# A hybrid attention layer on one core: the first projection step by token tile, and one output projection moved out of the merge

## The chip, the cores and the metric

The kernel runs on one core of a Trainium2 chip. The metric is the device time of one execution in microseconds (us), the median over the runs shown. The engines are TensorE (PE in the profile; its weight loads, which overlap its matmuls, are PEld), VectorE (DVE), ScalarE (ACT), GpSimd (POOL) and SyncE (SP), whose queue issues most of the loads. SBUF is the on-chip memory, PSUM the banks that TensorE writes.

## What is computed

One layer with two attention branches over 256 latent tokens (x) and 256 context tokens (ctx), width 2048, everything in fp32:

```python
hc = modulate(rms_norm(ctx, norm1_g), m_ctx[0], m_ctx[1])    # shift and scale from c_ctx
h  = modulate(rms_norm(x,   norm1_g), m_lat[0], m_lat[1])    # shift and scale from c
ka, va, kb, vb = keys and values of hc and of h, by w_in[:, :3072]
qa, qb, ga, gb = split_qg(h @ w_in[:, 3072:], q_norm_a, q_norm_b)
oa = gqa(qa, ka, va)                       # branch a: 16 heads of 128, 4 of keys
ob = diff_attn(qb, kb, vb, lam, ...)       # branch b: 8 heads, p0 - lam * p1
merged = sigmoid(ga) * (oa @ w_br_a) + sigmoid(gb) * (ob @ w_br_b)
x = x + m_lat[2] * (merged @ w_out)
x = x + m_lat[5] * swiglu(modulate(rms_norm(x, norm2_g), m_lat[3], m_lat[4]))
```

`m_lat` and `m_ctx` are six chunks of `silu(cond) @ w_ada + b_ada`. The scalar `lam` comes from four short vectors.

## The kernel before

**Products.** Each fp32 product is made of three fp32r products (`mm3`, L209): high part by high, high by low, low by high. `load_w` (L196) brings a weight tile of 256 rows by 512 columns (in the first steps 128 rows) through SP's queue into one of 7 buffers `wraw`; ScalarE casts the high part `whi` (L205), VectorE subtracts to get the low part `wlo` (L206). Activations are split in the same way (`split`, L214). One weight tile feeds 12 matmuls of 128x512 where there are two token tiles, 24 where there are four.

**The start.** The 512 tokens are four token tiles of 128 (indices 0 and 1 are the context, 2 and 3 are x). Each token tile lies in four column quarters `tok` of 512. The loads go in this order: x (both tiles at once, four DMAs), two small vectors, `w_ada` for the first shift and scale, the first weight tile, then the context (four DMAs). `row_norm` (L133) takes squares of the four quarters (for tiles 2, 3 and 0 on ScalarE, for tile 1 on VectorE), sums them and scales all four quarters by the root (the power is POOL's, L130). `ada_cond` (L249) makes shift and scale for a step by matmuls with 32 rows (L266) and a transpose (L275). `modulated` (L292) transposes a step's token columns (`xtp`, L306), applies scale and shift (`hx`), and splits. `kv_group` (L321) multiplies with `w_in`.

The key and value projection of all 512 tokens runs over six steps of 1, 1, 2, 4, 4 and 4 rows of tiles of `w_in` (`steps`, L492), and in each step over the six column groups 2, 3, 0, 4, 5, 1 (kb0, kb1, ka, vb0, vb1, va). In the first step both x tiles of column group 2 stand ahead, then both context tiles, then the other groups. The next step's shift and scale are made between the groups that `BATCH` (L491) names.

**Work on the side.** `later` (L468) makes the other chunks of the conditioning: per piece a load of 0.5 MB on SP's queue and a rank-one product on VectorE (`ada`, L364) that is ordered behind the latest `wlo`. `keys` and `values_a` normalise and rotate keys, and split values; `tables` (L174) makes the tables for the rotation and, at its end, the six operations for `lam` and `gsub`.

**Attention.** 16 units of branch b and 16 of branch a. A unit's front half makes scores and softmax, its back half the transposed probabilities and outputs. Between the halves `filler` (L703) feeds weight tiles of other projections, by `take` and by a count `pieces` of tiles against a goal (L744 and L752): six groups of q and eight groups of gates, whose results go to DRAM (`gate_d`) through POOL's queue. After every weight tile of the filler `side_work` (L692) does this:

```python
    turns[0] += 1
    if turns[0] % 2:
        take(later, 1)
    take(chores[-1], 1)
```

so that a piece of `later` comes every second tile, beside a piece of the chores (the keys of branch a and its values). The second tile of b's keys is made ahead of unit 8 (L734), with two tiles of filler per piece.

**The merge.** For each of four column groups (L760): the loads of b's two gates and their sigmoids, the projection of b's outputs (`w_brb`, 4 weight tiles), the loads of a's gates and sigmoids, the projection of a's outputs (`w_bra`, 8 weight tiles); `gated` (L781) multiplies and adds, `turn` (L782) transposes the sum. At each odd tile a piece of `later` is taken. The raw attention outputs are split by `o_parts` (L571), four heads at a time: for branch b (4, 5) ahead of the merge, for branch a (0 to 3) during it. Then follow `w_out`, the second norm and the feed-forward part, which the change does not touch.

## Time and profile before

| | |
|---|---|
| median of 3 runs | 1750.39 us (1748.45 to 1753.29) |
| the profiled execution, its own time | 1752.44 us |
| its span in the profile | 1750.7 us |
| TensorE busy | 1709.3 us, 98% of the span |
| VectorE, ScalarE, POOL busy | 1128.9 us (64%), 773.2 us (44%), 126.5 us (7%) |
| granted clock of TensorE, mean | 0.993 |
| DMA, mean over the span | 225 GB/s |

Busy time is the union of an engine's instructions over one span. The granted clock is the share of TensorE's full clock (1.00 is 2.4 GHz, 0.50 is 1.2 GHz). A matmul row's duration overlaps those of its neighbours in the pipeline, so the pace is read from the starts of two that follow each other. In brackets behind a row of the timeline stands the idle time ahead of it and what released the instruction. In the chain of work that ended last TensorE has 88%, VectorE 5%.

### The profile page before, as it was taken

Reading aid. Unit: us, or ns where it says so; the run is one execution under the profiler, and the core shown is the slowest. Engines: PE = TensorE matmul, PEld = TensorE weight load, DVE = VectorE, ACT = ScalarE, POOL = GpSimd, SP = SyncE. Lnnn points to the kernel's source line nnn. Section 1 sums busy time; section 2 is a strip of 40 time slices with the busy share of each in tenths; the row PEclk is TensorE's granted clock in tenths of the full one; section 3 lists DMA queues with packets and bytes.
Section 4 is the critical chain, followed back from the end, with each engine's and each line's share of the span. In section 5 each row is a group of like instructions: output and inputs, shape, how many; then the busy total and the mean of one; then the engine's idle time right before and its main releaser. Section 6 shows DMA issues by size and latency. Waiting matters only on the chain.

```text
span 1750.7 us, 21655 instructions
## 1 busy us (share of the span) xinstructions
PE 1709.3 (98%) x8106; PEld 1378.3 (79%) x8106; DVE 1128.9 (64%) x1416; ACT 773.2 (44%) x1061; POOL 126.5 (7%) x188
## 2 busy tenths in 40 slices
PE   5999999999999999999999999999999999999998
PEld 3767778887877788878888878888888888888887
DVE  4754658888798786968556664555566555454554
ACT  4422223246655566575444454444444444333332
POOL 2100001001132200001000100000000000000000
PEclk8999999999999999999999999999999999999999
DMA  9867785687776665648786756677777777666662
GB/s 271 281 222 262 239 306 181 195 269 246 223 231 222 204 236 175 212 133 278 245 288 225 251 176 190 203 239 233 238 239 239 234 237 232 208 197 214 219 204 90
DMA packets 190600, 393.47 MB, mean 225 GB/s; under 512 B 13120, under 2 KB 25488, under 8 KB 189984
## 3 DMA queue, kind: packets, MB, share of 16 engines
q1 hardware_dynamic: 183824, 369.71, 65.2%
q0 software_dynamic: 6672, 22.39, 4.1%
q8 instruction: 63, 1.03, 0.2%
q14 instruction: 41, 0.34, 0.1%
HBM read 383.62 MB, written 8.42 MB: 224 GB/s over the span
## 4 chain that ended last, share of the span: by engine, by line
PE 88%; DVE 5%; issue 3%; DMA 2%; ACT 1%; POOL 1%; SPq 1%; ACTq 0%; DVEq 0%; POOLq 0%
PE mm L211 27%; PE mm L210 26%; PE mm L212 26%; PE ada L266 2%; DVE wlo L206 1%; DMA wraw<-in_w_in_dram 1%; PE ptp L646 1%; PE s L626 1%; PE o L664 1%; ACT whi L205 1%; PE ftp L902 1%; DVE ada L364 0%; PE o L211 0%; DMA wada<-in_w_ada_dram 0%; PE o L210 0%
## 5 line engine op out<-in xcount | busy, mean ns | idle before, releaser
L206 DVE TENSOR_TENSOR wlo<-wraw,whi 128x1024 fp32r<-128x1024 f32 (+1 forms) x506 | 611.0, 1210 | 472.0 <-ACT whi L205 471.6
L205 ACT CAST whi<-wraw 128x1024 fp32r<-128x1024 f32 (+1 forms) x506 | 527.2, 1043 | 800.1 <-PE mm L212 685.4
L211 PE MATMUL mm<-wlo,hT 128*128 128x512 f32 x696 | 271.0, 389 | 2.0 <-DVE rstd L129 2.0
L210 PE MATMUL mm<-whi,hT 128*128 128x512 f32 x696 | 272.8, 392 | 0.0
L212 PE MATMUL mm<-whi,hT 128*128 128x512 f32 x696 | 271.2, 390 | 0.1
L210 PE MATMUL mm<-whi,xT 128*128 128x512 f32 x640 | 257.8, 407 | 2.3 <-ACT xT L215 1.8
L211 PE MATMUL mm<-wlo,xT 128*128 128x512 f32 x640 | 254.7, 398 | 4.9 <-DVE wlo L206 4.9
L212 PE MATMUL mm<-whi,xT 128*128 128x512 f32 x640 | 252.9, 395 | 0.0
L211 PEld LDWEIGHTS mm<-wlo,hT 128*128 128x128 f32 x696 | 130.7, 188 | 28.8 <-DVE wlo L206 2.4
L212 PEld LDWEIGHTS mm<-whi,hT 128*128 128x128 f32 x696 | 130.6, 188 | 27.7 <-DVE hT L216 0.5
L210 PEld LDWEIGHTS mm<-whi,xT 128*128 128x128 f32 x640 | 121.5, 190 | 39.3 <-issue 9.3
L364 DVE SCALAR_TENSOR_TENSOR ada<-wada,sc,ada 128x1024 f32<-128x1024 f32 x120 | 152.1, 1278 | 0.0
L210 PEld LDWEIGHTS mm<-whi,hT 128*128 128x128 f32 x696 | 130.7, 188 | 26.5
L211 PEld LDWEIGHTS mm<-wlo,xT 128*128 128x128 f32 x640 | 122.2, 191 | 30.5 <-DVE wlo L206 6.4
L212 PEld LDWEIGHTS mm<-whi,xT 128*128 128x128 f32 x640 | 122.0, 191 | 25.6
L210 PE MATMUL mm<-whi,fT 128*128 128x512 f32 x352 | 137.2, 390 | 0.0
L212 PE MATMUL mm<-whi,fT 128*128 128x512 f32 x352 | 137.0, 389 | 0.0
L211 PE MATMUL mm<-wlo,fT 128*128 128x512 f32 x352 | 136.9, 389 | 0.0
L210 PEld LDWEIGHTS mm<-whi,fT 128*128 128x128 f32 x352 | 66.1, 188 | 14.6 <-issue 0.8
L211 PEld LDWEIGHTS mm<-wlo,fT 128*128 128x128 f32 x352 | 66.1, 188 | 13.7
L212 PEld LDWEIGHTS mm<-whi,fT 128*128 128x128 f32 x352 | 66.1, 188 | 13.6
L210 PE MATMUL mm<-whi,cT 128*128 128x512 f32 x192 | 75.9, 395 | 0.4 <-ACT cT L215 0.4
(226 smaller groups left out, 2089.5 us busy)
## 6 DMA issues: line engine op xcount, KB each, us to landing
wada<-in_w_ada_dram SPq DMA_DIRECT2D x192, 512.0 KB, 4.5
wraw<-in_w_in_dram SPq DMA_DIRECT2D x154, 512.0 KB, 4.7
wraw<-in_w_ff_gate_dram SPq DMA_DIRECT2D x88, 512.0 KB, 4.2
wraw<-in_w_ff_up_dram SPq DMA_DIRECT2D x88, 512.0 KB, 4.1
wraw<-in_w_ff_down_dram SPq DMA_DIRECT2D x88, 512.0 KB, 4.8
wraw<-in_w_br_a_dram SPq DMA_DIRECT2D x32, 512.0 KB, 4.9
wraw<-in_w_out_dram SPq DMA_DIRECT2D x32, 512.0 KB, 5.2
wraw<-in_w_br_b_dram SPq DMA_DIRECT2D x16, 512.0 KB, 5.7
```

The lines of the kernel that those rows point to most:

```text
L205: nc.scalar.copy(out=hi[:, 0:nk], in_=raw[:, 0:nk])
L206: last_lo.append(nc.vector.tensor_tensor(out=lo[:, 0:nk], in0=raw[:, 0:nk], in1=hi[:, 0:nk].bitcast(F32), op=ALU.subtract))
L210: nc.tensor.matmul(ps, lhsT=ah, rhs=wh, start=first, stop=False)
L211: nc.tensor.matmul(ps, lhsT=ah, rhs=wl, start=False, stop=False)
L212: nc.tensor.matmul(ps, lhsT=al, rhs=wh, start=False, stop=last)
L266: nc.tensor.matmul(aps[32 * g:32 * g + 32, 0:ncol], lhsT=cst[:, k, :], rhs=rhs, start=(k < 4), stop=(k >= NKT - 4))
L364: nc.vector.scalar_tensor_tensor(out=dst, in0=wt, scalar=sc[:, 0, kt:kt + 1], in1=dst, op0=ALU.mult, op1=ALU.add)
L626: nc.tensor.matmul(sps[i], lhsT=qT[rows, x, hh, tk * P:(tk + 1) * P], rhs=kT["b", grp][y][rows, hh, :], start=(n == 0), stop=(n == 2))
L646: nc.tensor.transpose(out=tp[:, kt * P:(kt + 1) * P], in_=p[:, kt * P:(kt + 1) * P], identity=ident)
L664: nc.tensor.matmul(op[:, 0:BV], lhsT=pT[:, kt, :], rhs=vb[:, kt, hh * BV:(hh + 1) * BV], start=(kt == 0), stop=(kt == 3))
L902: nc.tensor.transpose(out=tp[:, j * P:(j + 1) * P], in_=act[tk][:, j * P:(j + 1) * P], identity=ident)
```

## The change

1. **Loads.** The two small vectors and `w_ada` go first; then each token tile by itself (four DMAs of 128x512), with weight tiles of groups 2, 3 and 0 between them.
2. **The first step by token tile.** `row_norm` now squares quarters 0 and 2 on ScalarE, 1 and 3 on VectorE, and returns the root; `row_scale` scales the quarters named: first only quarter 0, which the first step needs, and the others behind the split. `mod_first` transposes, modulates and splits one token tile; `kv_first` multiplies it with one of the column groups 2, 3, 0 and copies the result out. Groups 4, 5, 1 of the first step go as before. `BATCH[0]` is (3, 4) instead of (0, 2).
3. **Unread products.** `keep_busy` puts transposes of the identity into a PSUM bank that nobody reads: 16 before and 10 after the transposes of the first token tile, 8 and 10 around those of the second.
4. **`lambdas`.** The six operations for `lam` and `gsub` are ordered behind the `wlo` that is the latest when the fifth step begins.
5. **Side work.** A chore goes first; a piece of `later` only where there is no chore and no `quiet` (set while b's second keys are made), and then every second tile, every third once a's keys and values are done.
6. **The differential projection** (`w_br_b`) is no longer in the merge. It is the last part of the filler, behind the gates (`others`); its results go to DRAM (`prod_d`). The splits of b's outputs are done as it starts, those of a's first three groups behind a's units.
7. **The merge** has a's projection only. `load_gated` takes one step after each weight tile: it loads b's product, both gates, and puts the sigmoid behind the latest `whi`, the product of b's part behind the latest `wlo`. `later` is taken from the fifth tile on.

The parameter `BK` and the choice of PSUM bank by it go; no group used it at its value of 1000.

```diff
-    def load_tokens(src, i0):
+    def load_tokens(src, i):
...
-            nc.sync.dma_start(out=tok_in[q][:, i0:i0 + 2, :],
-                              in_=src[0, :, q * CG:(q + 1) * CG].rearrange("(i p) c -> p i c", p=P))
-
-    load_tokens(t["x"], 2)
+            nc.sync.dma_start(out=tok_in[q][:, i, :], in_=src[0, i % 2 * P:(i % 2 + 1) * P, q * CG:(q + 1) * CG])
...
-    def row_norm(i, on_act):
+    def row_norm(i):
...
-            if on_act:
+            if q % 2 == 0:
                 nc.scalar.activation(out=junk, in_=xt, func=AF.Square, accum_out=ssq[:, q:q + 1])
...
+    def keep_busy(n):
+        idle = mm_ps("idle")
+        with tc.issue_after(last_pe[0].ins):
+            for _ in range(n):
+                nc.tensor.transpose(out=idle[:, 0:P], in_=ident, identity=ident)
+
+    def mod_first(tok):
+        k0, nk = steps[0]
+        shift, scale = cond_of[k0]
+        w, c0 = (0, (tok - 2) * P) if tok >= 2 else (1, tok * P)
...
+        last_pe[0] = nc.tensor.transpose(out=tp[:, 0:P], identity=ident, in_=tok_in[0][:, tok, 0:P])
+        hx = scratch("hx")[:, 0:P]
+        v = xT.tile4(0) if w == 0 else cT_of[k0]
+        hi, lo = [v[:, x, 0, c0:c0 + P] for x in range(2)]
+        nc.vector.tensor_scalar(out=hx, in0=tp[:, 0:P], scalar1=scale[:, 0, w:w + 1], scalar2=shift[:, 0, w:w + 1], op0=ALU.mult, op1=ALU.add)
+        nc.scalar.activation(out=hi, in_=tp[:, 0:P], func=AF.Identity, scale=scale[:, 0, w:w + 1], bias=shift[:, 0, w:w + 1])
+        last_first.append(nc.vector.tensor_tensor(out=lo, in0=hx, in1=hi.bitcast(F32), op=ALU.subtract))
+        firsts[tok] = hi, lo
+
+    def kv_first(tok, cg):
+        (hi, lo), (wh, wl) = firsts[tok], ws0[cg]
+        nm, idx = kv_of[cg]
+        ps = mm_ps()
+        last_pe[0] = mm3(ps, hi, lo, wh[:, 0], wl[:, 0], True, True)
+        nc.scalar.copy(out=acc[nm][idx][:, tok * CG:(tok + 1) * CG], in_=ps)
...
-    BATCH = ((0, 2), (0, 2), (0, 1, 2, 3), (0, 1, 2, 3), (0, 1, 2, 3), ())
+    BATCH = ((3, 4), (0, 2), (0, 1, 2, 3), (0, 1, 2, 3), (0, 1, 2, 3), ())
     steps = [(0, 1), (1, 1), (2, 2), (4, 4), (8, 4), (12, 4)]
-    for i in (2, 3):
-        row_norm(i, True)
     drain(ada_cond(*steps[0]))
...
+    ws0 = {}
+    for tok, cgs in ((2, (2,)), (3, (3, 0)), (0, ()), (1, ())):
+        load_tokens(t["x"] if tok >= 2 else t["ctx"], tok)
+        for cg in cgs:
+            ws0[cg] = load_w(w_in, 0, cg * CG, 1)
+    for tok, todo in ((2, ((2, 2),)), (3, ((3, 2), (2, 3), (3, 3), (2, 0), (3, 0))), (0, ((0, 2), (0, 3), (0, 0))), (1, ((1, 2), (1, 3), (1, 0)))):
+        r = row_norm(tok)
+        row_scale(tok, r, (0,))
+        if tok >= 2:
+            keep_busy(16 if tok == 2 else 8)
+        mod_first(tok)
+        if tok >= 2:
+            keep_busy(10)
+        with tc.issue_after(last_first[-1].ins):
+            row_scale(tok, r, (1, 2, 3))
+        for of in todo:
+            kv_first(*of)
...
         if si == 4:
+            with tc.issue_after(last_lo[-1].ins):
+                lambdas()
             tables()
...
     def side_work():
-        turns[0] += 1
-        if turns[0] % 2:
-            take(later, 1)
-        take(chores[-1], 1)
+
+        if next(chores[-1], chores[-1]) is chores[-1] and not quiet:
+            turns[0] += 1
+            take(later, 1 if turns[0] % (3 if a_done else 2) else 0)
...
+    others = [(gate_d[w], xT, 0, w_in, (GA0, GB0)[w], cg) for w in range(2) for cg in range(4)]
+    n_gates = len(others)
+    others += [(prod_d, oT, AH, t["w_br_b"][0], 0, cg) for cg in range(4)]
...
+                dst, src, kt0, w, c0, cg = others.pop(0)
+                if kt0 and cg == 0:
+                    for g in (4, 5):
+                        o_parts(g)
+                for _ in project(w, src, BH if kt0 else NKT, c0 + cg * CG, to_dram(dst, cg), kt0=kt0, side=side_work):
...
+        if br == "a" and u % 4 == 2 and u > 4:
+            o_parts(u // 4 - 1)
...
+        def load_gated():
+
             for tk in range(2):
+                m.append(scratch(f"m{tk}"))
+                nc.gpsimd.dma_start(out=m[tk], in_=prod_d[tk, :, cg * CG:(cg + 1) * CG])
+                yield None
+                for w in (1, 0):
+                    g = scratch("gin", tag="p", bufs=4)
+                    nc.gpsimd.dma_start(out=g, in_=gate_d[w, tk, :, cg * CG:(cg + 1) * CG])
+                    yield None
+                    with tc.issue_after(last_hi[-1].ins):
+                        nc.scalar.activation(out=g, in_=g, func=AF.Sigmoid)
+                    if w == 1:
+                        with tc.issue_after(last_lo[-1].ins):
+                            nc.vector.tensor_tensor(out=m[tk], in0=m[tk], in1=g, op=ALU.mult)
+                gs.append(g)
+
+        def gated(tk, ps):
+            g = gs[tk]
+            nc.vector.tensor_tensor(out=g, in0=ps, in1=g, op=ALU.mult)
+            nc.vector.tensor_tensor(out=m[tk], in0=m[tk], in1=g, op=ALU.add)
+            after(2 + tk, turn(tk))
...
+        gates = load_gated()
+        for k, _ in enumerate(project(w_bra, oT, AH, cg * CG, gated)):
+            if k > 3:
+                take(later, 1)
+            if cg == 0 and k < 4:
+                on()
+                if k == 3:
+                    assert not work
+                    o_parts(3)
+            take(gates, 1)
```

Three places show how the instructions move. The first is TensorE in the first step, from the shift-and-scale products (`ada`, `atp`) to the first matmuls of column group 2 (`mm`); `xtp` is the transposed token tile, `idle` the bank of the unread products. Before:

```order
L266 MATMUL ada<-wada,cst 32x128 x24
L275 MATMUL atp<-ident,asb 128x128
L266 MATMUL ada<-wada,cst 32x128 x8
L275 MATMUL atp<-ident,asb 128x128
L306 MATMUL xtp<-ident,tok_89 128x128 x2
L210 MATMUL mm<-whi,xT_231 128x512
L211 MATMUL mm<-wlo,xT_231 128x512
L212 MATMUL mm<-whi,xT_231 128x512
```

In the change:

```order
L268 MATMUL ada<-wada,cst 32x128 x17
L277 MATMUL atp<-ident,asb 128x128
L268 MATMUL ada<-wada,cst 32x128 x15
L329 MATMUL idle<-ident 128x128 x4
L277 MATMUL atp<-ident,asb 128x128
L329 MATMUL idle<-ident 128x128 x12
L339 MATMUL xtp<-ident,tok_89 128x128
L329 MATMUL idle<-ident 128x128 x10
L212 MATMUL mm<-whi,xT_245 128x512
L213 MATMUL mm<-wlo,xT_245 128x512
L214 MATMUL mm<-whi,xT_245 128x512
L329 MATMUL idle<-ident 128x128 x8
```

One transposed token tile instead of two now stands ahead of the first three products; the unread products stand before and behind it, and again behind the products.

The second place is VectorE while the second tile of b's keys is made (`nr`, `sq`, `kbT`: norm, rotation and split of the keys; `on`: the output of a unit of branch b). Before:

```order
L206 TENSOR_TENSOR wlo<-wraw,whi 128x1024
L129 TENSOR_SCALAR rstdo<-sso 128x1
L401 TENSOR_REDUCE ss<-sq 128x8
L669 SCALAR_TENSOR_TENSOR on<-o,rstdo,gsub 128x128
L129 TENSOR_SCALAR rstd<-ss 128x8
L412 TENSOR_TENSOR sq<-kb_118,rp_kb 128x512
L206 TENSOR_TENSOR wlo<-wraw,whi 128x1024
L414 TENSOR_TENSOR nr<-nr,sq 128x8x32
L415 TENSOR_TENSOR nr<-nr,sq 128x8x32
L364 SCALAR_TENSOR_TENSOR ada_2851<-wada_4175,sc,ada_2851 128x1024
L416 TENSOR_TENSOR nr<-nr,rstd 128x512
L216 TENSOR_TENSOR kbT_4040<-ktp,kbT_4039 128x4x128
```

In the change:

```order
L208 TENSOR_TENSOR wlo<-wraw,whi 128x1024
L218 TENSOR_TENSOR kbT_4211<-ktp,kbT_4210 128x4x128
L127 TENSOR_SCALAR rstdo<-sso 128x1
L710 SCALAR_TENSOR_TENSOR on<-o,rstdo,gsub 128x128
L432 TENSOR_REDUCE ss<-sq 128x8
L127 TENSOR_SCALAR rstd<-ss 128x8
L443 TENSOR_TENSOR sq<-kb_114,rp_kb 128x512
L432 TENSOR_REDUCE ss<-sq 128x8
L445 TENSOR_TENSOR nr<-nr,sq 128x8x32
L446 TENSOR_TENSOR nr<-nr,sq 128x8x32
L208 TENSOR_TENSOR wlo<-wraw,whi 128x1024
L447 TENSOR_TENSOR nr<-nr,rstd 128x512
```

The product for the later conditioning (`ada`, L364 before) no longer stands among the parts of a key tile; the low parts of the weights stand there as before.

The third place is VectorE among the last units of branch a (`mx` and `rs` are the softmax's, `pT` the split of the probabilities, `oT` that of the attention outputs). Before:

```order
L216 TENSOR_TENSOR pT<-ptp,pT 128x4x128
L578 TENSOR_REDUCE mx<-s 128x1
L582 RECIPROCAL rs<-rs 128x1 x2
L578 TENSOR_REDUCE mx<-s 128x1
L216 TENSOR_TENSOR pT<-ptp,pT 128x4x128
L578 TENSOR_REDUCE mx<-s 128x1
L582 RECIPROCAL rs<-rs 128x1
L216 TENSOR_TENSOR pT<-ptp,pT 128x4x128
L578 TENSOR_REDUCE mx<-s 128x1
L582 RECIPROCAL rs<-rs 128x1 x2
L216 TENSOR_TENSOR pT<-ptp,pT 128x4x128 x2
L216 TENSOR_TENSOR oT_7045<-o_3466,oT_7045 128x1024
```

In the change:

```order
L208 TENSOR_TENSOR wlo<-wraw,whi 128x1024
L395 SCALAR_TENSOR_TENSOR ada_5539<-wada_7238,sc,ada_5539 128x1024
L208 TENSOR_TENSOR wlo<-wraw,whi 128x1024
L619 TENSOR_REDUCE mx<-s 128x1
L395 SCALAR_TENSOR_TENSOR ada_5539<-wada_7336,sc,ada_5539 128x1024
L623 RECIPROCAL rs<-rs 128x1
L619 TENSOR_REDUCE mx<-s 128x1
L218 TENSOR_TENSOR pT<-ptp,pT 128x4x128 x2
L623 RECIPROCAL rs<-rs 128x1
L218 TENSOR_TENSOR oT_7352<-o_6785,oT_7352 128x1024
L208 TENSOR_TENSOR wlo<-wraw,whi 128x1024 x2
L619 TENSOR_REDUCE mx<-s 128x1
```

Where units followed each other without a weight tile between them, low parts `wlo` and products `ada` now stand between them, and a split of outputs has moved in among them.

## Rows read from the trace of the kernel before

**Rows 1.** The page: busy time of each engine; the granted clock in 40 slices.
```profile
PE 1709.3 (98%) x8106; PEld 1378.3 (79%) x8106; DVE 1128.9 (64%) x1416; ACT 773.2 (44%) x1061; POOL 126.5 (7%) x188
...
PEclk8999999999999999999999999999999999999999
```

**Rows 2.** Windows by stage: length, busy us (count) by engine, granted clock, DMA share, GB/s.
```profile
0.00:40.00 40.00, 18.30 (x140) 11.64 (x141) 16.54 (x52) 16.21 (x40) 10.45 (x24) 0.87 0.98 266
40.00:400.00 360.00, 358.21 (x1762) 271.58 (x1761) 249.04 (x352) 110.17 (x150) 27.90 (x45) 1.00 0.73 243
400.00:800.00 400.00, 389.38 (x1974) 316.98 (x1974) 327.55 (x502) 248.46 (x446) 57.06 (x63) 0.98 0.64 209
```

**Rows 3.** Timeline, first step: start us, us, engine, line, instruction, [idle <-releaser].
```profile
13.48 0.16 DVE L144 TENSOR_REDUCE ss_row<-ss_part 128x1 f32<-128x4 f32 x1 [1.06 <-ACT junk L139]
...
14.59 1.67 DVE L148 TENSOR_SCALAR tok<-tok,rstd_row 128x512 f32<-128x512 f32 x4 [0.77 <-POOL rstd_row L130]
...
20.24 0.63 PE L306 MATMUL xtp<-ident,tok 128*128 128x128 f32 x2
...
22.67 0.80 PE L210 MATMUL mm<-whi,xT 128*128 128x512 f32 x1 [1.79 <-ACT xT L215]
...
23.27 0.69 DVE L141 SCALAR_TENSOR_TENSOR junk<-tok 128x512 f32<-128x512 f32 x1 [0.20 <-ACT junk L139]
...
38.67 0.63 PE L210 MATMUL mm<-whi,xT 128*128 128x512 f32 x1
...
39.10 0.63 PE L211 MATMUL mm<-wlo,xT 128*128 128x512 f32 x1
...
53.37 0.39 PE L212 MATMUL mm<-whi,cT 128*128 128x512 f32 x1
53.59 0.39 PE L210 MATMUL mm<-whi,xT 128*128 128x512 f32 x1
```

**Rows 4.** Windows at the lower granted clock, columns as in the second group.
```profile
29.50:39.70 10.20, 8.20 (x47) 5.69 (x48) 5.53 (x15) 3.57 (x7) 7.12 (x12) 0.50 0.96 192
...
497.20:500.50 3.30, 3.30 (x9) 2.65 (x8) 1.77 (x3) 0.63 (x1) 2.62 (x1) 0.50 0.76 191
...
780.50:783.80 3.30, 3.30 (x14) 3.11 (x14) 2.22 (x2) 3.27 (x5) 0.00 (x0) 0.50 0.30 97
```

**Rows 5.** Windows, the first 20 us.
```profile
0.00:10.00 10.00, 0.28 (x1) 0.18 (x1) 1.63 (x4) 3.03 (x6) 1.25 (x9) 1.00 0.69 211
10.00:20.00 10.00, 5.07 (x67) 2.83 (x67) 4.31 (x16) 4.39 (x15) 1.12 (x2) 1.00 1.15 323
```

**Rows 6.** Windows of four stretches of the middle, columns as before.
```profile
485.00:497.00 12.00, 9.71 (x48) 7.85 (x47) 11.89 (x22) 5.77 (x8) 4.59 (x3) 1.00 0.71 221
505.00:527.00 22.00, 21.40 (x102) 15.78 (x100) 21.21 (x38) 14.98 (x26) 5.94 (x6) 1.00 0.75 245
585.00:610.00 25.00, 21.71 (x108) 17.55 (x107) 21.00 (x38) 13.79 (x26) 3.13 (x4) 1.00 0.57 187
764.00:784.00 20.00, 16.55 (x93) 13.36 (x92) 11.80 (x21) 18.32 (x36) 2.23 (x4) 0.91 0.28 93
```

**Rows 7.** Timeline, TensorE at 480 us: four transposes of keys.
```profile
480.37 0.60 PE L433 MATMUL ktp<-ident,nr 128*128 128x128 f32 x4
```

**Rows 8.** Groups on VectorE from 475 to 613 us: count | busy us, mean ns.
```profile
L206 DVE TENSOR_TENSOR wlo<-wraw,whi 128x1024 fp32r<-128x1024 f32 x36 | 43.7, 1219 | 2.7 <-ACT whi L205 2.7
L364 DVE SCALAR_TENSOR_TENSOR ada<-wada,sc,ada 128x1024 f32<-128x1024 f32 x16 | 20.4, 1276 | 0.0
```

**Rows 9.** Timeline, VectorE: the first and the last of six such products.
```profile
483.90 1.28 DVE L364 SCALAR_TENSOR_TENSOR ada<-wada,sc,ada 128x1024 f32<-128x1024 f32 x1
...
521.31 1.28 DVE L364 SCALAR_TENSOR_TENSOR ada<-wada,sc,ada 128x1024 f32<-128x1024 f32 x1
```

**Rows 10.** Timeline, VectorE at 780 us: the differential outputs are split.
```profile
780.36 2.36 DVE L216 TENSOR_TENSOR oT<-o,oT 128x1024 fp32r<-128x1024 f32 x2
```

**Rows 11.** Instructions on the tile gin: its loads' time to landing.
```profile
DMA to landing us min/median/max: 3.2/4.6/6.8
```

More of the change, by code (lines that the diff above doesn't have):

```diff
@@ L703, in filler @@
     def filler():
-        while len(started) < len(q_order) or gates:
-            may = not gates or len(started) < 2 or a_done
+        while len(started) < len(q_order) or others:
+            may = not others or len(started) < 2 or a_done
             if may and len(started) < len(q_order) and len(started) - len(done) < 2:
@@ L720, in hybrid_block @@
     pieces = [0]
[L721 removed]
+    all_pieces = (len(q_order) + n_gates) * (NKT // WK) + 4 * (BH // WK)
     fill = filler()
```

100 lines of the change are left out of this document (31 added, 69 removed).

## The prediction

> **What bounds the kernel now.** I read the page first: TensorE is busy for 1709.3 of 1750.7 us and the granted clock stands at 0.9 or more in all but the first slice [rows 1]. So only TensorE's own waits, and the time it spends at the lower clock, can be won. Next the table by stage [rows 2], where the reader is to subtract TensorE's busy time from the length: 21.7 us are missing in the first 40 us, 10.6 us between 400 and 800 us, 1.8 us in the 360 us between. The two parts of the change lie in the first and the last of these three.
>
> The start in order of time [rows 3]: the first step's first matmul starts at 22.67 us, its 72nd and last at 53.37 us. In between the matmuls follow each other every 0.43 us while the granted clock is 0.50 (the 1.2 GHz level), every 0.22 to 0.23 us at 1.00 (2.4 GHz). The clock is at 0.50 from 29.5 to 39.7 us [rows 4]. DMA is not idle: 211 GB/s in the first 10 us, 323 GB/s in the next ten [rows 5].
>
> The middle: VectorE is the one that TensorE waits for. From 485 to 497 us it is busy for 11.89 of 12 us while TensorE loses 2.3; from 505 to 527 for 21.21 of 22 (TensorE loses 0.6); from 585 to 610 TensorE loses 3.3 [rows 6]. Between 764 and 784 us VectorE is busy for only 11.8 of 20, and TensorE loses 3.45: there the attention units stand behind each other with no projection between them. Four stretches of 3.4 us run at 0.50, two of them in [rows 4], the others at 528 and 610 us; such a stretch held 9 matmuls where the pace of 0.23 us gives 14, so each costs some 1.3 to 1.7 us. In all about 10 + 6 = 16 us are to be had in the middle.
>
> **The first step.** The change puts both small vector loads and the 2.1 MB for shift and scale ahead of x, then x and the context by tile of 128 tokens (1.05 MB each). By [rows 5] the first 2.1 MB take the first 10 to 11 us, and the next 1.05 MB at 323 GB/s 3.2 us: the first token tile is there at about 14 us. Of its four squares two are now on ScalarE; the last on VectorE ends 0.8 us later (0.69 and a read-out). From the row sum to the first scaled quarter it takes 1.1 us (13.48 to 14.59), the quarter itself 1.67 / 4 = 0.42. From the transposes to the first product it took 2.4 us (20.24 to 22.67); with 128 columns instead of 256, and one square of the next tile between on VectorE, I take 2.0. So the first product starts at 14 + 0.8 + 1.1 + 0.4 + 2.0 = 18.3 us, some 4 us earlier.
>
> After that VectorE's queue sets the pace of the tiles: three quarters still to scale (1.26), two squares (1.54), the row sum and power (1.1), the next tile's quarter (0.42), its modulated row and low part (128 columns each; I estimate 0.3, less than a quarter's 0.42 with its 512): 4.9 us a tile. The fourth tile is ready at 18.3 + 3 x 5 = 33.3 us. Behind it wait 9 + 36 matmuls at 0.23 = 10.3 us and 1 us of shift-and-scale products and transposes: step 0 ends at 44.6 us instead of 53.4. That is 8.8 us, of which I take **8**, since the second step's weights now arrive close to their use. The bounds are 4 (each tile 1.5 us later) and 11 (4.2 us a tile).
>
> The 44 added products that nobody reads cost TensorE 0.21 us each at the lower clock (two transposes in 0.63, the second 0.21 after the first [rows 3]) and 0.15 or less at the higher (four in 0.60 [rows 7]): 5 to 9 us in all. Sixteen lie in the wait for the first row sum, between the end of the shift-and-scale products and 16.3 us, the others in the 2 to 4 us that VectorE needs per tile; where ten of them (2.1 us) follow a transpose they outlast the 1.6 us to the low part by half a microsecond. I cost them at 1 us, within the bounds; if VectorE were ready earlier than I work out, they would stand on the path with up to 5 us.
>
> Taking the lambda arithmetic behind the weights of step 4 costs nothing on TensorE: five small VectorE operations and one on ScalarE, at a place where TensorE loses almost nothing. Its gain is a free VectorE queue during the first step; that is in the 8.
>
> **The filler and the merge.** The projection of the differential half (16 weight tiles, 192 matmuls) moves from the merge to the end of the filler. TensorE's work stays the same; ScalarE gets 8 copies and POOL 8 writes and 8 reads more, which lie beside matmuls on engines that are busy for 44 and 7% of the span [rows 1]. Two things are won. Where the keys are made, the rank-one products of the later conditioning (1.28 us each on VectorE, 16 between 475 and 613 us [rows 8]) no longer stand between the low parts of the weights. Six of them start between 483.9 and 521.3 us, around the first two stretches of [rows 6] (the first and the last in [rows 9]); in the new order none stands in VectorE's queue from the first such key tile to the last part of the values. That takes 6 x 1.28 = 7.7 us out of the queue where TensorE lost 2.9: those waits go, and with them two stretches at 0.50 (3 us). Between 585 and 610 us three stood (by the same view); at one in three instead of one in two one goes, 1.3 of the 3.3 us, and half the slow stretch, 0.8. Sum: 8.0 us. Second, the last units now have 24 matmuls each between them: the 3.45 us and their slow stretch (1.5) go, 5 us. Against it stands the conversion of the differential outputs, 2.36 us on VectorE [rows 10], which now falls between units: I cost 2 us. Middle: 8 + 5 - 2 = **11**, with bounds of 3 (only the last units, less the conversion) and 16 (all of it).
>
> The sum: 1752.4 - 8 - 11 = **1733** us against the profiled execution's own time; the median of the runs stands 2.0 us below that, which is within their spread, and I leave it. A measurement of this kernel can tell about 0.3%, 5.2 us, from no change.
>
> **A rule against it.** In the rows, nothing decides whether the unread products lift the clock: they are transposes, and before the change transposes stood at 1.00 only beside matmuls [rows 7] and, with 0.50, in the stretch from 780.5 us [rows 4]. The Trainium skill ("TensorE: Matmul & The Clock Gate", Part 4: PE-mode transpose) says that transposes do not count as a busy TensorE for the clock in the way matmuls do. By that rule the 0.50 would last into the real products; no row here shows it either way. My sum takes the higher level from the second tile on; by the other it is 3 us higher, as rival two has it.
>
> **The rivals.** *One: VectorE stays the bound in the middle.* The same norms, splits and low parts are in its queue; removing six products may only let other work fill it, and the products come back later at one per two or three weight tiles. For it: 21.21 of 22 us busy [rows 6], of which the products are under 4. Against: 7.7 us taken out against 2.9 lost. Then 5 us of the 11 stay: 1752.4 - 8 - 5 = 1739.
>
> *Two: the unread products do not lift the clock.* The 15 matmuls of the second tile then take 6.4 instead of 3.4 us, 1.4 over VectorE's 5 us, and the last tile's 9 take 1.8 more: 3 us, 1736.
>
> *Three: the start gains nothing and the middle only its last units.* The loads by tile bring row sums no earlier than the data do, and step 1's weights, still mixed with 2.1 MB of their own shift-and-scale weights, hold TensorE instead: 1752.4 - 4 = 1748. For it: DMA at 323 GB/s is near what it showed at its best in these rows. Against: after 40 us TensorE alone set the pace (358.21 of 360 us busy [rows 2]), so the loads had room.
>
> *Four, on the other side: the merge waits for its gates.* Each of 16 sigmoids now stands in ScalarE's queue among the weight casts, one or two weight tiles (12 matmuls of 0.23, 2.75 us each) behind its load's issue. A gate's load lands after 3.2 to 6.8 us [rows 11]. Where it lands later than 2.75 plus the two tiles of casts that run ahead (8.2 us in all), TensorE waits for the difference, 16 times. At 9.7 us that is 24 us: 1733 + 24 = 1757, slower. Against: 6.8 was the longest of 16, and one POOL queue served them then as now. For: POOL now has the products' writes in front of the first gates, and the sums on VectorE wait for a second load each.
>
> **How the numbers follow.** Forecast 0.50, rival one 0.19, two 0.16, three 0.08, four 0.07. The first three are all faster by over 0.3%: 0.85; rival three is the same, 0.08; four is slower, 0.07. The range runs from 1725 (both upper bounds, 11 and 16) to 1747 (both lower bounds, 4 and 3, give 1745, and a run of the same kernel differs by 2); it leaves out rivals three and four.
>
> **What would show it.** Right: the first product near 18 us; step 0's last near 45 us; between 485 and 527 us no VectorE wait over 1 us and no clock of 0.50; between 740 and 800 us TensorE busy throughout; the busy time between 400 and 800 us within 5 us of the length. Wrong: the granted clock still at 0.50 after 30 us (rival two); TensorE waiting for weights between 45 and 60 us (three); a wait for the gates' loads on ScalarE that shows on TensorE in the merge (four); VectorE full and low parts late between 480 and 610 us (one).

## The result and the profile after

The changed kernel takes 1732.41 us (1731.48 to 1732.81, 4 runs) against 1751.09 for the kernel before, timed beside it, a ratio of 0.9891 with a 95% interval of 0.9879 to 0.9903: 18.7 us faster, where 19 were forecast. The profiled execution has a span of 1730.7 us, 20.0 below that of before. The sum came out, its terms less so: the start gave less than I took and the middle more.

The page of the changed kernel, the lines of [rows 1]:

```profile
PE 1706.1 (99%) x8150; PEld 1378.5 (80%) x8150; DVE 1132.6 (65%) x1428; ACT 775.0 (45%) x1063; POOL 135.5 (8%) x204
...
PEclk9999999999999999999999999999999999999999
```

Windows by stage of the changed kernel, then the four stretches of [rows 6] (length, busy us of PE, PEld, DVE, ACT, POOL, granted clock, DMA share, GB/s):

```profile
0.00:40.00 40.00, 27.61 (x194) 20.90 (x195) 21.41 (x64) 19.86 (x45) 11.10 (x24) 0.96 0.96 266
40.00:400.00 360.00, 358.40 (x1780) 270.83 (x1773) 254.03 (x359) 107.44 (x146) 27.95 (x45) 1.00 0.74 246
400.00:800.00 400.00, 397.04 (x2032) 324.90 (x2031) 336.38 (x505) 251.98 (x446) 57.78 (x65) 1.00 0.71 230
...
485.00:497.00 12.00, 12.00 (x62) 9.77 (x61) 9.87 (x16) 6.01 (x12) 2.57 (x3) 1.00 0.53 175
505.00:527.00 22.00, 22.00 (x109) 17.41 (x108) 20.54 (x35) 14.75 (x24) 7.29 (x6) 1.00 0.66 192
585.00:610.00 25.00, 24.03 (x119) 18.59 (x118) 23.86 (x38) 14.12 (x29) 3.62 (x3) 1.00 0.66 213
764.00:784.00 20.00, 20.00 (x107) 17.05 (x106) 16.30 (x22) 14.34 (x25) 1.08 (x2) 1.00 0.88 304
```

Between 400 and 800 us TensorE now misses 3.0 us instead of 10.6, and the granted clock is 1.00 throughout. In the first 40 us it is busy for 9.3 us more, but that counts the unread products too. (The granted clock reads 1.00 from 13.1 to 16.5 us as well, although the unread products there follow each other every 0.21 us, the pace of the lower level; in the run without unread products it reads 1.00 from 24.4 to 29.5 us with matmuls every 0.43 us. Ahead of a trace's first change of level the pace has to be read instead.) What was won at each point is better read from the starts of the same matmul in both timelines:

| start of, us | before | change | start alone | rest alone | lambda early | lambda alone |
|---|---|---|---|---|---|---|
| the first key and value product | 22.67 | 18.85 | 18.72 | 22.60 | 18.84 | 22.64 |
| the 72nd | 53.37 | 47.69 | 46.45 | 52.63 | 53.47 | 52.84 |
| the 144th (end of the second step) | 74.82 | 70.64 | 69.44 | 74.35 | 75.45 | 74.63 |
| the 1152nd (the last) | 345.65 | 339.84 | 339.74 | 344.55 | 348.03 | 347.44 |
| the first product with hT (after the merge) | 1010.77 | 989.42 | 1000.89 | 993.96 | 997.17 | 1010.31 |

(The last four columns are experiments below.) The change stands 4.2 us ahead after two steps, 5.8 after all six, 21.35 after the merge, 20.0 at the end. So in this pair of traces the middle gave 21.35 - 5.8 = 15.5 us, and 1.35 were lost again behind the merge. (Of the 5.8, 1.6 fell in behind the second step: TensorE waited 1.7 us there before, 1.1 of it behind a late load around 247 us, and 0.2 here. The run without unread products, whose start differs little, waits there too, at 244 us, so I don't count that to the change.)

One pair of traces says less than it seems to. From the 1152nd product to the first with hT the three traces with the old middle (before, start alone, lambda alone) take 665.1, 661.2 and 662.9 us; the change and rest alone take 649.6 and 649.4. So the middle is worth 11.6 to 15.7 us, and the 15.5 lie near the upper end. Five traces have the same start as the change (the change, start alone, and below old side work, old place, no quiet): in them the 72nd product starts between 46.45 and 47.99 us, the 144th between 69.44 and 70.75, the 1152nd between 339.55 and 341.69. Two have the old one (before, rest alone). By these the start is worth 3.6 to 5.4 us after two steps and 2.9 to 6.1 after six.

The first step on TensorE in the changed kernel (start us, us, engine, line, operation; in brackets the idle time ahead and what ended it):

```profile
14.27 2.61 PE L329 MATMUL idle<-ident 128*128 128x128 f32 x12
17.52 0.31 PE L339 MATMUL xtp<-ident,tok 128*128 128x128 f32 x1 [0.65 <-DVE tok L148]
17.67 1.25 PE L329 MATMUL idle<-ident 128*128 128x128 f32 x10
18.85 0.50 PE L212 MATMUL mm<-whi,xT 128*128 128x512 f32 x1
...
19.64 1.03 PE L329 MATMUL idle<-ident 128*128 128x128 f32 x8
23.06 0.30 PE L339 MATMUL xtp<-ident,tok 128*128 128x128 f32 x1 [2.38 <-DVE tok L148]
23.20 2.12 PE L329 MATMUL idle<-ident 128*128 128x128 f32 x10
24.98 0.77 PE L212 MATMUL mm<-whi,xT 128*128 128x512 f32 x1
...
31.18 0.50 PE L212 MATMUL mm<-whi,cT 128*128 128x512 f32 x1 [1.55 <-ACT cT L344]
...
34.65 0.50 PE L212 MATMUL mm<-whi,cT 128*128 128x512 f32 x1 [0.21 <-ACT cT L344]
```

Twelve unread products take 2.61 us, ten at 17.67 only 1.25: the clock rose between them, after TensorE had done nothing but transposes since 13.15 us. Behind the 2.4 us wait ahead of the second tile it was at 0.50 again, and the next ten take 2.12. Windows on either side of that fall:

```profile
16.60:23.40 6.80, 3.77 (x28) 3.00 (x27) 5.92 (x16) 3.64 (x10) 1.21 (x2) 1.00 1.05 388
23.40:26.80 3.40, 3.40 (x14) 3.04 (x13) 3.26 (x12) 1.23 (x4) 0.00 (x0) 0.50 1.13 332
```

The fall is not the rule. Of the six traces with this same wait (2.4 us), three have it (the change, old side work, no quiet) and three go on at 1.00 (start alone, old place, lambda early). The same window in start alone:

```profile
23.40:26.80 3.40, 3.40 (x20) 2.78 (x19) 3.26 (x12) 2.50 (x6) 0.00 (x0) 1.00 1.13 332
```

That is why start alone and old place reach the 72nd product 1.2 us earlier than the change, at 46.45 and 46.47 us.

What VectorE does between two tiles' first quarters (timeline of VectorE):

```profile
16.89 0.49 DVE L148 TENSOR_SCALAR tok<-tok,rstd_row 128x512 f32<-128x512 f32 x1 [0.77 <-POOL rstd_row L128]
17.29 0.69 DVE L208 TENSOR_TENSOR wlo<-wraw,whi 128x512 fp32r<-128x512 f32 x1
...
22.43 0.49 DVE L148 TENSOR_SCALAR tok<-tok,rstd_row 128x512 f32<-128x512 f32 x1 [0.45 <-POOL rstd_row L128]
22.83 0.68 DVE L208 TENSOR_TENSOR wlo<-wraw,whi 128x512 fp32r<-128x512 f32 x1
```

From quarter to quarter it is 5.54 us, not 4.9: my list of VectorE's work per tile had no weight's low part in it.

### The profile page after: what moved, and what is told of

Its sections match the earlier page's. It is cut to its first block, busy times and chain, and to the rows that moved or that the text cites. A ratio compares the mean times of both kernels' runs of the same rounds, so it can differ in the third digit from the quotient of the medians.

```text
span 1730.7 us, 21827 instructions
## 1 busy us (share of the span) xinstructions
PE 1706.1 (99%) x8150; PEld 1378.5 (80%) x8150; DVE 1132.6 (65%) x1428; ACT 775.0 (45%) x1063; POOL 135.5 (8%) x204
## 4 chain that ended last, share of the span: by engine, by line
PE 88%; DVE 5%; issue 3%; DMA 1%; ACT 1%; POOL 1%; SPq 0%; DVEq 0%; ACTq 0%; POOLq 0%
PE mm L212 26%; PE mm L213 26%; PE mm L214 26%; PE ada L268 2%; DVE wlo L208 1%; PE ptp L687 1%; PE o L705 1%; DMA wraw<-in_w_in_dram 1%; PE ftp L951 1%; PE s L667 1%; ACT whi L207 1%; PE o L213 0%; PE o L214 0%; PE o L212 0%; PE s L212 0%
## 5 line engine op out<-in xcount | busy, mean ns | idle before, releaser
L212 PEld LDWEIGHTS mm<-whi,fT 128*128 128x128 f32 x352 | 66.1, 188 | 14.5 <-issue 0.8
L214 PEld LDWEIGHTS mm<-whi,fT 128*128 128x128 f32 x352 | 66.1, 188 | 13.9
L213 PEld LDWEIGHTS mm<-wlo,fT 128*128 128x128 f32 x352 | 66.1, 188 | 13.4
```

What stands on the lines that cost most here:

```text
L212: nc.tensor.matmul(ps, lhsT=ah, rhs=wh, start=first, stop=False)
L213: nc.tensor.matmul(ps, lhsT=ah, rhs=wl, start=False, stop=False)
L214: return nc.tensor.matmul(ps, lhsT=al, rhs=wh, start=False, stop=last)
```

## The experiments

Each run was timed beside runs of the kernel before; those had medians of 1750.4 to 1752.0 us. Times of different rows are best compared by their ratios and intervals.

| run | median us | ratio to before (95% interval) |
|---|---|---|
| the change | 1732.41 | 0.9891 (0.9879 to 0.9903) |
| start alone | 1748.23 | 0.9986 (0.9977 to 0.9995) |
| rest alone | 1737.71 | 0.9925 (0.9913 to 0.9938) |
| old side work | 1741.51 | 0.9944 (0.9932 to 0.9957) |
| old place of the projection | 1736.01 | 0.9911 (0.9897 to 0.9924) |
| no quiet | 1735.54 | 0.9908 (0.9888 to 0.9928) |
| lambda alone | 1751.70 | 1.0007 (0.9998 to 1.0016) |
| lambda early | 1738.14 | 0.9930 (0.9917 to 0.9943) |
| no unread products | 1733.35 | 0.9900 (0.9886 to 0.9914) |
| 30 unread products | 1732.73 | 0.9900 (0.9886 to 0.9914) |
| late scaling | 1734.24 | 0.9906 (0.9892 to 0.9920) |
| early conditioning | 1733.59 | 0.9904 (0.9889 to 0.9919) |
| early conditioning, two steps | 1735.95 | 0.9924 (0.9909 to 0.9939) |

My theory was that start and middle are separate, the start bound by VectorE's queue and the middle won by taking the rank-one products away from the keys and by filling the last units. The rivals stand in each expectation.

**Start alone** (side work, filler and merge of before put into the change).

> Start alone: loads, first step by token tile, unread products and lambdas as in the change; side work, filler and merge as before. Theory (the two parts are separate, each worth what its landmarks in the two traces show): the 144th key and value product stands near 70.6 us (74.82 before, 70.64 in the change) and the kernel ends 4 to 6 us earlier than before, 1745 to 1747, with TensorE's waits between 490 and 610 us and between 764 and 784 us all still there. Rival (an earlier start only shifts the weights' loads, and the middle's waits grow by what the start won): within 1.5 us of before. Rival (the start is worth the 8 us forecast, and part of it is lost in the middle of the change): 1743 or less.

It gained 2.5 us (0.9 to 4.0 by the interval), between theory and the first rival, and neither is ruled out. Its profiled execution was the fastest of 11 (1742.64 to 1751.44), so its column above is not the median's. In it the start is all there, and the old waits of the middle too:

```profile
PE mm L213 <- DVE wlo L208: 4.5, 5, 2.3
PE ptp L687 <- ACT junk_o L708: 1.9, 1, 1.9
PE s L667 <- ACT p L622: 1.2, 3, 0.6
```

(Waits of TensorE from 480 to 620 us: sum, times, longest. Before, the first line was 4.4 us in 3.)

**Rest alone** (the kernel before with the change's side work, filler and merge).

> The rest alone: side work, filler and merge as in the change; loads, first step and the lambda arithmetic as before. Theory (separate parts): 15 us less than before, 1735 to 1737, the first product 22.7 us, and no clock of 0.50 between 480 and 800 us. Rival (the middle's gain needs the start, since later products are taken earlier there): 1740 or more.

13.0 us less than before, some 2 short of theory, and nearer to it than to the rival. The clock is nowhere at 0.50 between 480 and 800 us, as theory said. So the start is worth 5.3 us on top of the rest, and 2.5 by itself. Whether these two really differ is not shown: the three intervals together leave about 3 us open.

**Old side work.**

```diff
-        if next(chores[-1], chores[-1]) is chores[-1] and not quiet:
-            turns[0] += 1
-            take(later, 1 if turns[0] % (3 if a_done else 2) else 0)
+        turns[0] += 1
+        if turns[0] % 2:
+            take(later, 1)
+        take(chores[-1], 1)
```

> The change with the side work of before: a later piece at every second weight tile beside a chore, also while b's second keys are made; the differential projection stays the last filler. Theory (VectorE's queue with the rank-one products is what TensorE waited for while keys are made): VectorE waits of 1 to 3 us and two to three stretches at 0.50 come back between 480 and 615 us, the last units stay filled; 6 to 10 us more than the change, 1738 to 1743. Rival (more filler between units alone ends the waits, the rule adds nothing): within 2 us of the change, 1732 to 1735.

9.1 us more than the change, the time that theory gave. Its mechanism is only in part what the trace shows. Waits of TensorE from 480 to 620 us, first in this run, then in the change:

```profile
PE s L667 <- DVE adac_sb L413: 2.2, 1, 2.2
PE mm L213 <- DVE wlo L208: 1.4, 3, 0.6
PE s L667 <- ACT p L622: 0.9, 2, 0.7
PE ktp L464 <- DVE nr L447: 0.4, 1, 0.4
```

```profile
PE o L705 <- DVE kaT L218: 0.7, 1, 0.7
PE mm L213 <- DVE wlo L208: 0.6, 1, 0.6
PE s L667 <- ACT p L622: 0.3, 1, 0.3
```

4.9 against 1.6 us, and one stretch at 0.50 (at 570 us) came back in this trace, not the two or three that I expected. The waits for low parts are 1.4 us in all. The longest wait, with the slow stretch behind it, is not for a rank-one product: VectorE itself stood still for a small load of the later conditioning (a bias), and a unit's scores waited for the operation behind that load:

```profile
567.48 0.69 DVE L413 TENSOR_TENSOR adac_sb<-adac,adac_sb 128x512 f32<-128x512 f32 x1 [3.52 <-DMA adac_sb<-in_b_ada_dram]
```

So what is shown is that the old side work costs 9.1 us, not that the rank-one products do it.

**Old place of the projection** (filler and merge of before in the change, with the new side work).

> The change with the differential projection back in the merge and the merge of before; the new rule for side work stays. Theory: the waits between 480 and 615 us stay away, those of the last units come back with their stretch at 0.50 (3.5 + 1.5 us, forecast less 2 for the conversion): 3 to 6 us more than the change, 1735 to 1739. Rival (the new merge with its spread loads is what won, through waits in it that the rows before hide): 8 us more or above. Rival (the conversion among the last units eats what the filler wins): within 2 us of the change.

3.6 us more, the time that theory gave; the intervals overlap by a little, but the four executions (1734.50 to 1737.05) all lie above the change's four. Waits from 735 to 800 us, the two largest of this run and the one of the change:

```profile
PE o L212 <- DVE pT L218: 2.3, 2, 1.3
PE s L212 <- ACT p L622: 0.4, 1, 0.4
```

```profile
PE mm L214 <- DVE oT L218: 1.3, 1, 1.3
```

The last units' waits are back, 3.2 us in all; what the change has in their place is one wait for the conversion of the outputs, which I had priced at 2 us. The stretch at 0.50 did not come back: start alone and lambda alone have the same waits there without it too, and of these four traces only the kernel before has it.

Undone one at a time the two edits cost 9.1 + 3.6 = 12.7 us, undone together (start alone against the change) 15.8; the intervals don't tell these apart. But the traces show one place where the edits overlap. TensorE from 480 to 530 us, while b's second keys are made, in the kernel before, start alone, old side work, old place and no quiet (the next run):

```profile
480.00:530.00 50.00, 46.57 (x212) 35.73 (x211) 45.78 (x76) 28.52 (x47) 18.18 (x11) 0.94 0.66 207
480.00:530.00 50.00, 44.93 (x216) 34.71 (x215) 47.12 (x79) 26.89 (x45) 16.87 (x10) 1.00 0.68 211
480.00:530.00 50.00, 49.29 (x239) 39.38 (x238) 45.37 (x69) 29.04 (x47) 16.77 (x13) 1.00 0.76 241
480.00:530.00 50.00, 49.88 (x248) 39.96 (x247) 45.31 (x81) 32.35 (x55) 14.29 (x12) 1.00 0.60 178
480.00:530.00 50.00, 49.39 (x241) 39.57 (x241) 46.28 (x75) 30.04 (x47) 18.73 (x13) 1.00 0.71 223
```

With both edits undone TensorE misses 3.4 and 5.1 us there. With only the old side work it misses 0.7, although six of the rank-one products stand in VectorE's queue again (482 to 515 us); with only the old place it misses 0.1. So either edit alone ends the first waits in these traces, and the products alone do not bring them back. How the longer filler does it is open.

**No quiet** (the line that sets `quiet` left out).

> The change without its quiet: while b's second keys are made, a later piece may be taken at every second weight tile, as far as no chore stands ahead of it; all else as in the change (the side work of before in whole cost 9.1 us). Theory (as the prediction had it: six of the products, 7.7 us of VectorE, stood among the first waits, which with two stretches at 0.50 were worth 5.9 of 8 us): VectorE waits of TensorE come back between 480 and 530 us, 4 to 7 us more than the change, 1736.5 to 1739.5. Rival (the products among a's keys and values, which a chore first keeps away here too, were the costly ones): within 2 us of the change, waits near 500 us under 1 us in all.

Inconclusive: by the ratios it is 3 us behind the change, and the intervals overlap. In its trace four of the products stand between 485 and 510 us, and TensorE's waits for weights from 480 to 620 us are 1.4 us in all, the longest 0.8, so the first waits of before did not come back with the products there. But the traced execution was the fastest of five by 4.4 us (1730.16; the others 1734.51 to 1736.96), so it cannot say what the 3 us of the others are. Which part of the side work's rule is worth the 9 us stays open.

**Lambda early, lambda alone** (the order behind the fifth step's weights taken out of the change; put alone into the kernel before).

```diff
-            with tc.issue_after(last_lo[-1].ins):
-                lambdas()
+            lambdas()
```

> The change with the lambda arithmetic not ordered behind the fifth step's weights: it stands in VectorE's queue in the second step again, where it waits for its own small loads. Theory (VectorE's queue sets the pace of the first steps): VectorE waits there for a load as long as before (4.0 us at 36 us) or somewhat less, since the loads are issued behind the last root, and the low parts behind it come late: 144th product 1 to 4 us later than 70.6 us, and the time as much. Rival (nothing waits behind it for long, VectorE has room after 36 us): 144th product within 0.5 us of 70.6.

> The kernel before with one edit: the six lambda operations ordered behind the fifth step's weights, as in the change. With the early lambda arithmetic the change lost its whole gain at the start (144th product 75.5 us, against 70.6). Theory (in the kernel before, VectorE's wait for the small loads lay beside matmuls at the lower clock, TensorE did not wait; the two edits only win together): 144th product within 1 us of 74.8, the time within 2 us of before. Rival (the order of the lambda arithmetic is the start's whole gain, the token tiles give nothing): 144th product 70 to 72 us, time 1745 to 1748.

Early, it costs 5.7 us by the medians and 4.8 at the 144th product, more than theory's 4; its time is that of rest alone (1738.14 and 1737.71). VectorE's row, and TensorE's behind it:

```profile
39.65 0.23 DVE L187 TENSOR_SCALAR gsub<-gsub 128x128 f32<-128x128 f32 x1 [4.63 <-DMA gsub<-in_subln_g_dram]
```

```profile
41.09 0.80 PE L213 MATMUL mm<-wlo,xT 128*128 128x512 f32 x1 [4.38 <-DVE wlo L208]
```

During this wait the granted clock fell; it was at 0.50 from 39.2 to 46.1 us, a cost that theory did not have.

Alone it gains nothing (theory): before the change VectorE waited 4.01 us in the same place, and TensorE was still busy there with matmuls at 0.43 us. The token tiles win nothing clear of noise with that wait, and the order wins nothing without them.

**No unread products** (`keep_busy` returns at once).

> The change without the 44 unread products. Theory (they lift the clock: in the change's trace it is at 1.00 from 16.6 us, when TensorE had done nothing but such products and one transpose since 13.2 us): the clock stays at 0.50 at least through the 18 products of the x tiles (3 + 15 at 0.43 us, where 8 of them took that long in the change) and into the context tiles; less some 0.3 us by which the second tile's products start earlier; the kernel is 2 to 4 us slower than the change, 1734.5 to 1736.5, and its 72nd product comes 2 to 4 us later than 47.7 us. Rival (transposes don't count for the clock, it rose through the products before them, or it makes no difference): 72nd product within 0.5 us of 47.7, time within 1 us of the change. Rival (they stood on the path): 72nd product before 47 us.

The 72nd product comes at 48.61 us, 0.9 later, between theory and the first rival (0.6 to 2.2 later than in the five traces with the change's start), and the medians differ by 0.9 too, which the intervals don't tell from nothing. The clock rose late, though not as late as theory said; the twelfth, thirteenth and fifteenth of the second tile's products:

```profile
29.31 0.47 PE L214 MATMUL mm<-whi,xT 128*128 128x512 f32 x1
29.62 0.40 PE L212 MATMUL mm<-whi,xT 128*128 128x512 f32 x1
...
30.09 0.39 PE L214 MATMUL mm<-whi,xT 128*128 128x512 f32 x1
```

Until 29.3 us they follow each other every 0.43, then every 0.23. But the context tiles wait for VectorE in either kernel, which hides most of it.

**30 unread products** instead of 8 ahead of the second tile's transpose.

> The change with 30 unread products instead of 8 between the first x tile's products and the second tile's transpose (the wait from 20.4 to 23.1 us, behind which the clock was at 0.50 for 3.4 us). Theory (that wait let the clock fall): the clock stays at 1.00; ten unread products at 0.11 instead of 0.21 and five products at 0.23 instead of 0.43 us bring the end of the second tile's products from 29.4 to 27.5 to 28.2 us; the third tile then waits for VectorE, so the 72nd product comes 0.3 to 1.5 us earlier. Rival (the clock falls all the same at this place): no change or up to 2 us later, as 22 more products then stand in the way.

As theory said, the clock stays at 1.00 here: ten products at 23.31 us take 1.25, and the 72nd product starts 0.9 us earlier (46.77). That the wait made it fall is likely and not shown: three of six traces with the wait keep 1.00 as well, and of the four with 20 or 30 unread products there, which have no wait, none falls. Against the traces without the fall (46.45 and 46.47) the 30 products win nothing. The 144th starts 2.5 us later (73.16). ScalarE and TensorE in the second step:

```profile
61.93 2.03 ACT L207 CAST whi<-wraw 128x512 fp32r<-128x512 f32 x3 [9.21 <-DMA wraw<-in_w_in_dram]
```

```profile
62.60 0.75 PE L212 MATMUL mm<-whi,xT 128*128 128x512 f32 x1 [2.21 <-ACT whi L207]
```

In the change the same wait is 0.57 us. Behind the longer wait here the clock was at 0.50 from 62.7 to 66.1 us. What TensorE won in the first step of this execution it handed to a wait for the second step's weights; in start alone, as early at the 72nd product, that wait is 0.5 us and the 144th comes at 69.44.

**Late scaling** (quarters 1 to 3 scaled behind the fourth tile, 20 unread products; the four roots get a tile of their own, which the diff leaves out).

```diff
-        with tc.issue_after(last_first[-1].ins):
-            row_scale(tok, r, (1, 2, 3))
+        rows_r[tok] = r
         for of in todo:
             kv_first(*of)
+    with tc.issue_after(last_first[-1].ins):
+        for tok in (2, 3, 0, 1):
+            row_scale(tok, rows_r[tok], (1, 2, 3))
```

> The change with the scaling of quarters 1 to 3 (1.27 us of VectorE per token tile) put behind the fourth tile's low part, and 20 instead of 8 unread products ahead of the second tile's transpose. Theory (VectorE's queue sets the pace of the token tiles, 5.5 us in the change): the second tile's products start 1.0 to 1.8 us earlier than 24.98, the fourth's up to 3 us earlier than 34.65; 72nd product 43.5 to 46.5 us; 1 to 4 us faster than the change unless the second step's weights hold it. Rival (the loads by tile set the pace): second and fourth tile within 0.5 us of the change.

VectorE's pace was what held the second tile: from first quarter to first quarter it is 3.95 us instead of 5.54. The second tile's products start at 23.69 us (1.3 earlier), the fourth's at 32.48 (2.2 earlier); about half of that is the clock, which did not fall here, for against start alone (24.25 and 33.43) it is 0.6 and 1.0. The 72nd comes at 46.60, just later than theory's range. The end of the second step does not move (144th at 70.39), and the time is no better. ScalarE's queue stands behind a cast that waits for its load, with a result's copy behind it that TensorE's next group needs:

```profile
49.57 0.62 ACT L210 CAST whi<-wraw 128x512 fp32r<-128x512 f32 x1 [2.61 <-DMA wraw<-in_w_in_dram]
50.09 0.58 ACT L379 COPY va<-mm 128x512 f32<-128x512 f32 x1
```

**Early conditioning** (late scaling, and `next(nxt1)` behind each context tile, with `nxt1` the second step's `ada_cond`, and `BATCH[0]` empty; in the second run also the third step's first part at the end of the first step).

> Late scaling and 20 unread products as in the run before (144th product 70.4 us there), and in addition the second step's shift and scale made between the context tiles, their loads ahead of the first step's last three weight tiles. Theory (behind the faster token tiles the second step's weights bind: 7 load buffers, four of them held by shift-and-scale weights from 27 to 44 us until TensorE's products, DMA near idle from 33 to 38 us): buffers come free earlier, 144th product 66 to 69 us, time 1 to 4 us below the change, 1728.5 to 1731.5. Rival (the first step's last weight tiles then come late, and TensorE waits there what it wins later): 144th product 70 us or later.

> As the run before, and the third step's first shift-and-scale products taken at the end of the first step as well (in the change their four buffers are held from 44 to 51 us). Theory (held buffers): no wait of TensorE for loads over 0.5 us between 45 and 70 us, 144th product 0 to 1.5 us earlier than in the run before. Rival (these loads now stand ahead of the second step's first weights): a wait of 1 us or more between 45 and 55 us, 144th product later than in the run before.

Neither theory's forecast of the 144th product held: it starts at 72.56 and 73.84 us. In the first run the rival won: TensorE waits 1.4 us for a weight's high part at 37.9 us and 2.0 behind a copy at 50.9 us. The premise of an idle DMA was wrong as well: from 33 to 38 us of late scaling its engines moved only 122 GB/s but were busy for a share of 1.00. In the second run the wait that the rival named, between 45 and 55 us, is not there; TensorE waits 4.6 us ahead of 42.8 us, for the third step's shift-and-scale weights themselves, whose products now stand in its queue. No order of these loads that I tried beats the change.

## Why the prediction came out

- **First product:** 18.3 forecast, 18.85 measured. Right in sum; two terms miss in opposite ways: the row sum came at 15.78 us instead of 14.8, and from the transpose to the product it took 1.33 us (17.52 to 18.85) instead of 2.0.
- **Pace of the token tiles:** 4.9 us forecast, 5.54 measured. The step that failed is the list of VectorE's work: it left out the low parts of the weights (0.69 us each).
- **End of the first step:** 44.6 forecast, 47.69 measured. The fourth tile came 1.35 us late (34.65 for 33.3). In the traces without the fall it comes at 33.43 to 33.55, so that most of the 1.35 is the clock; that the slower pace does not show there is luck, since the fourth tile follows the third after 3.75 us and not after 5. Behind it I allowed 1 us beside the 45 matmuls; from 34.65 to 47.69 us it was 13.04 less 10.3, that is 2.7 (and as much in start alone). This is the term that was mis-sized.
- **"That is 8.8 us, of which I take 8":** mis-sized. 5.7 at the 72nd product, 4.2 at the 144th, just above my lower bound of 4. The stretch between these two is 1.5 us longer than before, of which TensorE's waits for weights, my reason for a discount, are 0.8; by three experiments such waits are the next bound.
- **Lambda arithmetic, "that is in the 8":** right, but its price was never worked out. Without it the rest of the start wins nothing clear of noise.
- **Unread products (rival two):** they did lift the clock at the first tile, against the rival: without them the first tile's products run at 0.43 us and the clock rises only at 29.3 us. In three of six traces it then fell for some 3.4 us ahead of the second tile's products, which no case of the prediction had. Their worth at the 72nd product is 0.6 to 2.2 us by the traces; the time does not tell it from nothing. The Trainium skill's rule ("TensorE: Matmul & The Clock Gate", Part 4) does not hold for these transposes: by the rows above the clock rose while only transposes ran.
- **Middle:** 11 forecast, 15.5 measured in this pair of traces, 11.6 to 15.7 by all of them, 13.0 by the median of rest alone. The terms' sizes were 8 for the keys (9.1 by the undone side work) and 5 - 2 for the last units (3.6 by the undone place). The mechanism of the first term is not borne out: the sum took the waits of the first keys for the work of six products and gave them to the side work alone, but with the products back and the longer filler in place TensorE misses 0.7 us there, and what the old side work brings back lies later. In both terms the slow stretches (3, 0.8 and 1.5 us) were priced as certain; with nearly the same waits the kernel before has four, lambda alone three and start alone one.
- **Merge (rival four):** did not come. The gates' loads land later than before (3.2, 4.6 and 6.8 us in [rows 11]):

```profile
DMA to landing us min/median/max: 3.7/5.0/8.0
```

But the longest, 8.0 us, is below the rival's 8.2, and the only waits of TensorE from 735 to 1000 us are these:

```profile
PE mm L213 <- DVE wlo L208: 2.0, 1, 2.0
PE mm L214 <- DVE oT L218: 1.3, 1, 1.3
PE o L213 <- DVE pT L218: 0.3, 1, 0.3
```

- **Rival one** (5 of 11 us in the middle) is refuted by the 11.6 to 15.7, although its premise came true: other work did fill VectorE (20.54 of 22 us from 505 to 527). **Rival three** (4 us in all) is refuted by the 18.7; but its mechanism, the second step's weights, is what held the start in the experiments above.

So that 1733 was met within a microsecond is luck: in this pair of traces two errors nearly cancel, 2.2 us too much at the start (5.8 of 8 even at the last key and value product) and 4.5 too little in the middle, with the 1.35 us lost behind the merge. By the medians of start alone and rest alone the start is worth 2.5 to 5.3 us and the middle 13.0 to 15.8: too much at the start and too little in the middle as well.

## What to carry to other kernels

When the bound of a stage moves, list every instruction in the queue that becomes the bound, the weights' conversions too, and then look at what is late next: here it was the loads, and what four experiments tried on the start was given back within one step. A wait that costs nothing because it lies beside slow work becomes the whole cost once that work is fast, so two edits can be worth something only together. Size each part by taking it out of the finished kernel and also by trying it alone, and look in the traces for waits that either part ends by itself, as from 480 to 530 us here: such a wait belongs to neither part alone. And a price that comes from one trace, of a slow stretch above all, has to be looked for in a second trace of the same code before it is counted on.

## What was not expected of the hardware

The loss behind the merge is a stretch at 0.50 after TensorE's wait for VectorE (2.0 us) among the first products with hT, in the changed kernel:

```profile
996.20:999.60 3.40, 3.40 (x11) 2.65 (x11) 2.74 (x4) 0.00 (x0) 0.37 (x1) 0.50 0.84 296
```

The kernel before has the same wait (2.0 us at 1014 us) and no such stretch. Of the 14 traces of this study, all with that wait, four have it: the change, rest alone, old place, early conditioning. From the first product with hT to the end these four take 741.1 to 741.6 us, the other ten 739.8 to 740.0. The same holds for the 2.4 us wait ahead of the second token tile (three of six traces) and for the waits of the last units (one of four). So the same wait is followed by the lower clock in one execution and not in another, and some 1.4 us of a difference between two single traces can be that alone.
